# A hybrid backbone on one Trainium2 core: RMS norms folded into the transposes as diagonal products, two gathers' buffers exchanged, two steps moved, one add given to TensorE

## The chip, the cores and the metric

The kernel runs on one core of one Trainium2 chip. The metric is device time in microseconds from start to end of the program. All arithmetic is in 32-bit floats (fp32); the kernel's matrix products run either on fp32 operands or on pairs of fp32r operands (a rounded high part and a low part, three products per pair).

## The reference, cut to what matters

Two layers over 256 latent and 256 context tokens of width D = 1024. Each layer: a modulated RMS norm, one input projection that feeds three mixers, an output projection, a second modulated norm, and a mixture of 16 experts with two experts per token. In layer 1 the context tokens only feed the mixers.

```python
def rms_norm(x, g):
    return x * lax.rsqrt(jnp.mean(x * x, axis=-1, keepdims=True) + EPS) * g

for l in range(2):
    mod = jnp.split(silu(c) @ w_ada[l] + b_ada[l], 6)
    h  = rms_norm(x,  norm1_g[l]) * (1 + mod[1]) + mod[0]
    o  = token_mixers(h @ w_in[l], ...) @ w_out[l]
    x  = x + mod[2] * o
    h2 = rms_norm(x, norm2_g[l]) * (1 + mod[4]) + mod[3]
    x  = x + mod[5] * moe(h2)
```

The same is done to the context stream with `c_ctx` for `c`. The change touches `h`, the first norm of a layer, and in layer 1 what lies just ahead of it: the end of layer 0's experts, `x + mod[5] * moe(h2)`.

## The kernel before, in words

**Tiles.** The 512 tokens are four tiles of 128 (T = 0 to 3; 0 and 1 are latent, 2 and 3 context), held in SBUF as `X[T]`, 128 tokens by 1024 channels. To multiply by `w_in`, the channels must lie on the partitions, so each tile's eight 128x128 blocks (k-slices, ko = 0 to 7) are turned by TensorE.

**Opening of a layer.** `normed` (L397) goes over the tiles: ScalarE squares and sums the tile (L389), GpSimd (POOL) makes the mean plus epsilon (L391; in layer 0 VectorE does that) and its power -1/2, `rstd` (L394), and ScalarE writes the scaled tile `X * rstd` (L404) into the buffers `V` (tiles 0, 1), `UG` and `U`. `modulated` (L428) takes two k-slices of all four tiles: TensorE transposes them through `tr` (L181) into a PSUM tile `T`, ScalarE scales and shifts by the modulation (L440), VectorE casts the result to `big` and writes the low part (L190, L199). Then, per k-slice, `parts` splits the weight slice into `wsp` (ScalarE L189, VectorE L199) and 18 products (`mm3`, L157) add into the PSUM tiles `A`. This loop over ko (L455 to L485) makes the S5 and Fourier columns of the projection; in layer 1 it calls `modulated` at ko = 0 and 4, for two pairs of slices each, and loads half of the weight slices (`wload`, L303, 1 MB per half, on SP's DMA queue).

**Fillers.** `self.fill` is a generator of steps of `ada` (L306): each step k loads 1 MB of `w_ada` (L317) and multiplies it with the conditioning, four products into `E`. In layer 1 steps k < 5 load through GpSimd's queue, the later ones through SP's. The code calls `next(fill)` at set places: here in `ready(T)` of `combine0` (L1792), that is before each tile's norm (2, 1, 1, 1 steps), and in the ko loop after ko = 5.

**End of layer 0's experts.** In `experts0` each token's two expert rows are gathered from DRAM by GpSimd (L1684, two gathers of 0.5 MB per tile) into four buffers `rg[T]`; the order of the gathers in the code is T = 0, 1, 2, 3. The buffers come from three pools: `ws2`, the two `bm` buffers, and `ws`, the pool of four 1 MB buffers that also serves `w_in` and `w_ada`. Tile 3's is in `ws`. `others` (L1633 to L1637) and `back` then put gathered rows and modulated sums together; `back` is TensorE products of `y` with `OG`. The last loop (L1780) multiplies each tile's two PSUM halves `acc[T][n]` by the modulation `B5` and adds them to `X[T]` (L1789, L1790). For tile 3 VectorE first adds the gathered rows (L1788).

**What sets the order.** The Tile framework's scheduler places the instructions of each engine by its own model, apart from the stretches that `issue_after` and `chain` tie down; a buffer that is taken again from a pool makes its load wait for the last reader of the old contents. So an engine's order follows from program order, pools and that model together.

Of the kernel before, what the change touches and what calls it, by code (L numbers as in the profile page):

```python
# [19 lines left out]
P = 128  # L20
D = 1024
# [113 lines left out]
class Net:  # L135
# [261 lines left out]
    def normed(self, ready=None, pool=None):  # L397

        xv = self.t(self.mix, [P, 2, D], "V")
        self.xn = [xv[:, 0, :], xv[:, 1, :], self.t(self.mix, [P, D], "UG"), self.t(self.mix, [P, D], "U")]  # L400
        for T in range(4):
            if ready:
                ready(T)
            self.nc.scalar.activation(self.xn[T], self.X[T], AF.Copy, scale=self.rstd(T, pool=pool))  # L404


    def mixers(self, l, sa, sb):
# [20 lines left out]
        def modulated(kp):  # L428
            for s in range(2):
                xn = self.xn[2 * s:2 * s + 2]  # L430
                pt = t(self.psT, [P, 2, 256], "T")
                for i in range(2):
                    ko = 2 * kp + i
                    for sh in range(2):
                        self.tr(pt[:, i, sh * P:sh * P + P], xn[sh][:, ko * P:ko * P + P])
                f = t(self.tmp, [P, 2, 256], "w2")
# [19 lines left out]
        for ko in range(8):  # L456
# [21 lines left out]
            if both:  # L478
                if ko in (0, 2, 4):
                    next(self.first)  # L480
                    next(self.first)
                elif ko > 5:
                    next(fill)
            elif ko in (5,):
                next(fill)  # L485
# [1103 lines left out]
    def experts0(self, st):  # L1589
# [76 lines left out]
        for e in range(NE):  # L1666
# [12 lines left out]
            if e == NE - 1:  # L1679

                rg = [t(p, [P, 2048], "w").rearrange("p (k n) -> p k n", k=2) for p in (self.ws2, *self.bm, self.ws)]
                for T in range(4):
                    for k in range(2):
# [96 lines left out]
        for T in range(4):  # L1780
            if T == 3:
                back(0, 3)
            back(1, T)
            for n in range(2):
                c = slice(n * 512, n * 512 + 512)
                w = t(self.tmp, [P, 512], "w2")
                if T == 3:
                    nc.vector.tensor_add(w, acc[T][n], rg[T][:, 0, c])  # L1788
                nc.vector.tensor_mul(w, w if T == 3 else acc[T][n], B5[T // 2][:, c])  # L1789
                nc.vector.tensor_add(self.X[T][:, c], self.X[T][:, c], w)  # L1790

    def combine0(self):  # L1792

        def ready(T):
            for _ in range((2, 1, 1, 1)[T]):
                next(self.fill)
# [208 lines left out]
```

## Time and profile before

| What | us |
|---|---|
| median of 3 runs | 1094.84 |
| their range | 1093.45 to 1096.46 |
| time of the profiled execution | 1093.7 |
| its span, first to last instruction | 1091.9 |
| layer 0's opening | 0 to 63 |
| layer 0's mixers and routing | 63 to 340 |
| layer 0's experts | 340 to 640 |
| layer 1's opening, up to the next projection | 640 to 682 |
| layer 1's mixers and routing | 682 to 860 |
| layer 1's experts | 860 to 1092 |

TensorE (PE) is busy 1022.4 us (94% of the span), its weight loads (PEld) 649.7, VectorE (DVE) 598.1 (55%), ScalarE (ACT) 305.7 (28%), GpSimd (POOL) 164.0 (15%). The mean granted TensorE clock is 0.973 of full speed. A row of the timeline gives the start of an instruction or a run of like ones, their time and their count; in brackets stands how long the engine had been idle, and what released it. Ends of pipelined products overlap the next start, so a price is best read from start to start. An fp32 product counts as two records, a transpose as one.

### The profile page before, as it was taken

To read this page: it belongs to the slowest core of one execution; us is meant where nothing else is said; L and a number is where in the kernel's file an instruction comes from. 1 tells how busy PE (TensorE), PEld (TensorE's weight loads), DVE (VectorE), ACT (ScalarE), POOL (GpSimd) and SP (SyncE) were. 2 spreads that over 40 slices of the span, in tenths; PEclk is the share of its full clock that TensorE was granted. 3 is DMA by queue.
4 is the path that set the end of the run, shared out by engine and by line. 5 is a ranking of instruction groups with operands and counts; after the bars stand their busy time and mean duration, and the time that the engine had idled before them with its cause. 6 is when DMAs were issued, how large, how long until landed. Compare 5 with 4: busy or idle time off the path is not lost.

```text
span 1091.9 us, 21030 instructions
## 1 busy us (share of the span) xinstructions
PE 1022.4 (94%) x8468; PEld 649.7 (59%) x8468; DVE 598.1 (55%) x1675; ACT 305.7 (28%) x623; POOL 164.0 (15%) x259
## 2 busy tenths in 40 slices
PE   4999998989997999799999979999999999999997
PEld 2667676547895666465655528767658555555553
DVE  8987946657851322378663376784468423232232
ACT  5323234655101111010112244322373221111111
POOL 3101143001222321211111330113010000000000
PEclk9999999999977999999999998998999899999999
DMA  9867557757297999999999948634868999999991
GB/s 328 289 244 191 215 224 299 227 199 290 78 346 254 343 390 372 396 362 394 378 387 411 374 166 229 222 121 168 287 226 292 337 410 403 406 406 407 410 388 47
DMA packets 109121, 325.25 MB, mean 298 GB/s; under 512 B 10688, under 2 KB 19232, under 8 KB 104400
## 3 DMA queue, kind: packets, MB, share of 16 engines
q1 hardware_dynamic: 94016, 275.62, 68.3%
q0 software_dynamic: 14272, 46.96, 12.9%
q8 instruction: 71, 1.16, 0.4%
q10 hardware_dynamic: 720, 1.17, 0.3%
q14 instruction: 42, 0.34, 0.1%
HBM read 305.32 MB, written 18.38 MB: 296 GB/s over the span
## 4 chain that ended last, share of the span: by engine, by line
PE 43%; DMA 17%; DVE 4%; issue 3%; ACT 1%; POOL 1%; SPq 0%; ACTq 0%; DVEq 0%; POOLq 0%
DMA w<-in_w_up_dram 14%; PE g L157 13%; PE A L157 11%; PE D L157 7%; PE E L157 3%; PE u L157 3%; PE y L157 3%; PE T L181 2%; DMA w<-in_w_down_dram 1%; PE T L157 1%; DMA w<-in_w_ada_dram 1%; POOL qr L754 1%; PE T L1876 1%; DVE E L811 0%; ACT E L817 0%
## 5 line engine op out<-in xcount | busy, mean ns | idle before, releaser
L157 PE MATMUL A<-wsp,big 128*128 128x512 f32 (+1 forms) x720 | 163.8, 375 | 3.2 <-DVE big L190 2.1
L157 PE MATMUL g<-w,xt 128*32 128x384 f32 (+1 forms) x1280 | 149.5, 450 | 5.5 <-PEq L1533 3.2
L157 PEld LDWEIGHTS A<-wsp,big 128*128 128x128 f32 x720 | 122.8, 191 | 40.4 <-ACT wsp L189 7.5
L157 PE MATMUL u<-w,xt 128*32 128x384 f32 (+1 forms) x1024 | 121.2, 463 | 4.6 <-DMA w<-in_w_up_dram 4.6
L157 PEld LDWEIGHTS g<-w,xt 128*32 128x32 f32 x1280 | 68.1, 110 | 50.5 <-issue 26.6
L157 PE MATMUL g<-w,x 128*64 128x512 f32 x368 | 94.1, 595 | 0.0
L157 PE MATMUL y<-w,H 128*32 128x384 f32 (+1 forms) x1152 | 88.4, 456 | 5.7 <-issue 5.0
L157 PE MATMUL E<-w,CS 128*32 128x512 f32 (+1 forms) x448 | 60.4, 566 | 21.3 <-DMA w<-in_w_ada_dram 21.2
L157 PEld LDWEIGHTS y<-w,H 128*32 128x32 f32 x1152 | 52.8, 111 | 39.0 <-issue 18.0
L1946 DVE TENSOR_TENSOR cst<-cst,g 64x512 f32<-64x512 f32 x16 | 11.1, 691 | 117.6 <-ACT cst L1945 117.6
L199 DVE TENSOR_TENSOR wsp<-w,wsp 128x512 fp32r<-128x512 f32 x64 | 43.8, 687 | 50.8 <-ACT wsp L189 49.7
L157 PEld LDWEIGHTS u<-w,xt 128*32 128x32 f32 x1024 | 55.4, 111 | 25.8 <-ACT s L1714 2.9
L189 ACT ACTIVATE wsp<-w 128x512 fp32r<-128x512 f32 x64 | 40.2, 631 | 103.0 <-PE A L157 90.2
L157 PE MATMUL A<-w,big 128*128 128x512 f32 (+1 forms) x224 | 66.0, 386 | 0.0
L189 ACT ACTIVATE y<-y 96x384 f32<-96x384 f32 (+2 forms) x34 | 17.5, 516 | 155.2 <-PE y L157 99.8
L157 PEld LDWEIGHTS g<-w,x 128*64 128x64 f32 x368 | 29.9, 137 | 45.6 <-issue 42.2
L1709 DVE TENSOR_TENSOR s<-s,u 96x384 f32<-96x384 f32 x16 | 8.8, 551 | 85.0 <-ACT s L1708 85.0
L1618 POOL DMA_DIRECT2D xg<-G x60 | 32.6, 549 | 132.2 <-DVE xt L1625 77.9
L1901 DVE SCALAR_TENSOR_TENSOR y<-D,gs,ba 64x256 f32<-64x256 f32 x62 | 30.0, 483 | 38.2 <-PE D L157 37.4
L157 PE MATMUL D<-w,WO 128*64 128x256 f32 x384 | 47.2, 382 | 0.5 <-ACT WO L189 0.5
L157 PEld LDWEIGHTS A<-w,big 128*128 128x128 f32 x224 | 40.1, 188 | 7.6 <-issue 0.5
L157 PEld LDWEIGHTS D<-w,WO 128*64 128x64 f32 x384 | 28.7, 137 | 15.9 <-issue 2.6
(420 smaller groups left out, 1692.5 us busy)
## 6 DMA issues: line engine op xcount, KB each, us to landing
w<-in_w_gate_dram SPq DMA_DIRECT2D x110, 512.0 KB, 12.5
w<-in_w_up_dram SPq DMA_DIRECT2D x110, 512.0 KB, 12.4
w<-in_w_down_dram SPq DMA_DIRECT2D x55, 1024.0 KB, 12.6
w<-in_w_ada_dram SPq DMA_DIRECT2D x27, 1024.0 KB, 6.9
w<-in_w_in_dram SPq DMA_DIRECT2D x14, 1024.0 KB, 5.0
w<-in_w_ada_dram SPq DMA_DIRECT2D x32, 256.0 KB, 6.0
w<-in_w_ada_dram SPq DMA_DIRECT2D x16, 512.0 KB, 4.7
w<-in_w_out_dram SPq DMA_DIRECT2D x8, 1024.0 KB, 6.5
```

The source lines that it names most:

```text
L157: self.pe = self.pl = self.nc.tensor.matmul(out, lhsT, rhs, start=start, stop=stop)
L181: self.pl = self.nc.tensor.transpose(out, in_, self.ident[:n, :n])
L189: return self.nc.scalar.activation(out, in_, AF.Copy)
L199: self.lo = self.nc.vector.tensor_tensor(lo, x, hi.bitcast(F32), op=OP.subtract)
L754: nc.gpsimd.tensor_tensor(r, v, self.neghalf[:, 0:8], op=OP.pow)
L1618: q.dma_start(xg[blk(g)], rows[g])
L1709: nc.vector.tensor_mul(s[:cap, :], s[:cap, :], pg[1][:cap, 0:384])
L1876: nc.tensor.transpose(pt[:, k, :], s[64:P, k * P:k * P + P], self.ident[64:P, 64:P])
L1901: nc.vector.scalar_tensor_tensor(y[o:o + 64, m, b, :], py[m][q, :], gs[q, e % 2:e % 2 + 1], B5[q, m, :], op0=OP.mult, op1=OP.mult)
L1946: nc.vector.tensor_mul(s[64:P], s[64:P], pg[64:P])
```

## The change

There are five edits, in one diff:

1. `normed` no longer makes scaled tiles. GpSimd makes four diagonals `dg[T] = ident * rstd(T)`, 128x128 each, in the buffer `U`.
2. `modulated` replaces each transpose of a scaled block by an fp32 product of the block `X[T]` with `dg[T]`, which transposes and scales at once: 32 per layer, in both layers.
3. `ready(T)` takes one filler step for T = 0, 1, 2 and none for T = 3; the ko loop takes one after ko = 2, 4 and 6. In all there are six, as before.
4. Tile 2's gathered rows go to `ws` and tile 3's to the second `bm` buffer; the gathers are issued in the order 0, 1, 3, 2 of the code.
5. Tile 3's gathered rows are added in PSUM by two TensorE products with the identity, 128x512 each, instead of two VectorE adds.

```diff
--- before.py
+++ after.py
@@ -396,12 +396,12 @@
 
     def normed(self, ready=None, pool=None):
 
-        xv = self.t(self.mix, [P, 2, D], "V")
-        self.xn = [xv[:, 0, :], xv[:, 1, :], self.t(self.mix, [P, D], "UG"), self.t(self.mix, [P, D], "U")]
+        dg = self.t(self.mix, [P, 4, P], "U")
+        self.dg = [dg[:, T, :] for T in range(4)]
         for T in range(4):
             if ready:
                 ready(T)
-            self.nc.scalar.activation(self.xn[T], self.X[T], AF.Copy, scale=self.rstd(T, pool=pool))
+            self.nc.gpsimd.tensor_tensor(self.dg[T], self.ident, self.rstd(T, pool=pool).to_broadcast([P, P]), op=OP.mult)
 
 
     def mixers(self, l, sa, sb):
@@ -427,12 +427,12 @@
 
         def modulated(kp):
             for s in range(2):
-                xn = self.xn[2 * s:2 * s + 2]
                 pt = t(self.psT, [P, 2, 256], "T")
                 for i in range(2):
                     ko = 2 * kp + i
                     for sh in range(2):
-                        self.tr(pt[:, i, sh * P:sh * P + P], xn[sh][:, ko * P:ko * P + P])
+                        T = 2 * s + sh
+                        self.mm(pt[:, i, sh * P:sh * P + P], self.X[T][:, ko * P:ko * P + P], self.dg[T], True, True)
                 f = t(self.tmp, [P, 2, 256], "w2")
                 for i in range(2):
                     ko = 2 * kp + i
@@ -481,7 +481,7 @@
                     next(self.first)
                 elif ko > 5:
                     next(fill)
-            elif ko in (5,):
+            elif ko in (2, 4, 6):
                 next(fill)
         for T in range(4):
             self.cp(UT[:, T // 2, :, T % 2, :], pu[T // 2][:, T % 2, :].rearrange("p (g c) -> p g c", c=16))
@@ -1678,8 +1678,8 @@
                 xg = gather(e + 2)
             if e == NE - 1:
 
-                rg = [t(p, [P, 2048], "w").rearrange("p (k n) -> p k n", k=2) for p in (self.ws2, *self.bm, self.ws)]
-                for T in range(4):
+                rg = [t(p, [P, 2048], "w").rearrange("p (k n) -> p k n", k=2) for p in (self.ws2, self.bm[0], self.ws, self.bm[1])]
+                for T in (0, 1, 3, 2):
                     for k in range(2):
                         nc.gpsimd.indirect_dma_start(out=rg[T][:, k], out_offset=None, in_=self.Y,
                                                      in_offset=bass.IndirectOffsetOnAxis(ap=self.gi[:, k, T:T + 1], axis=0))
@@ -1780,19 +1780,19 @@
         for T in range(4):
             if T == 3:
                 back(0, 3)
+                for n in range(2):
+                    self.mm(acc[3][n], self.ident, rg[3][:, 0, n * 512:n * 512 + 512], False, False)
             back(1, T)
             for n in range(2):
                 c = slice(n * 512, n * 512 + 512)
                 w = t(self.tmp, [P, 512], "w2")
-                if T == 3:
-                    nc.vector.tensor_add(w, acc[T][n], rg[T][:, 0, c])
-                nc.vector.tensor_mul(w, w if T == 3 else acc[T][n], B5[T // 2][:, c])
+                nc.vector.tensor_mul(w, acc[T][n], B5[T // 2][:, c])
                 nc.vector.tensor_add(self.X[T][:, c], self.X[T][:, c], w)
 
     def combine0(self):
 
         def ready(T):
-            for _ in range((2, 1, 1, 1)[T]):
+            if T < 3:
                 next(self.fill)
         self.normed(ready, self.fin)
         self.finx.close()
```

**TensorE, layer 1's opening, before.** `y<-y,OG` is the last product of `back`; `E` are the filler steps (x4 is one step), `T` the transposes, `A` the projection.

```order
L157 MATMUL E_10218<-w_10221,CS_95 32x512 x4
L157 MATMUL E_10218<-w_10227,CS_95 32x512 x4
L157 MATMUL E_10218<-w_10241,CS_95 32x512 x4
L181 MATMUL T_10295<-cst_5_87,V_10215 128x128 x4
L157 MATMUL E_10218<-w_10255,CS_95 32x512 x4
L181 MATMUL T_10305<-cst_5_87,UG_10216 128x128
L181 MATMUL T_10315<-cst_5_87,V_10215 128x128 x4
L157 MATMUL E_10218<-w_10269,CS_95 32x512 x4
L181 MATMUL T_10305<-cst_5_87,U_10217 128x128
L181 MATMUL T_10305<-cst_5_87,UG_10216 128x128
L181 MATMUL T_10305<-cst_5_87,U_10217 128x128
L157 MATMUL A_10289<-wsp_2072_10335,big_2054_10284 128x256
```

The same place after the change, first up to the first `A`:

```order
L157 MATMUL y_2016_10144<-w_10009,cst_5_87 128x512
L157 MATMUL y_2017_10145<-w_10009,cst_5_87 128x512
L157 MATMUL y_2016_10144<-y_10134,OG_9715 128x512
L157 MATMUL y_2017_10145<-y_10134,OG_9715 128x512
L157 MATMUL E_10214<-w_10217,CS_95 32x512 x4
L157 MATMUL E_10214<-w_10231,CS_95 32x512 x4
L157 MATMUL E_10214<-w_10245,CS_95 32x512 x4
L157 MATMUL T_10279<-U_10213,X_1_66 128x128 x4
L157 MATMUL T_10289<-U_10213,X_2_67 128x128
L157 MATMUL T_10299<-U_10213,X_1_66 128x128 x4
L157 MATMUL A_10273<-wsp_2066_10319,big_2048_10268 128x256
```

Eleven `A` products on, at the last `A` of ko = 1 for tiles 0 and 1:

```order
L157 MATMUL A_10273<-wsp_2068_10341,big_2049_10269 128x256
L157 MATMUL E_10214<-w_10385,CS_95 32x512 x4
L157 MATMUL E_10214<-w_10477,CS_95 32x512 x4
L157 MATMUL T_10289<-U_10213,X_2_67 128x128 x3
L157 MATMUL T_10309<-U_10213,X_2_67 128x128 x4
```

The products with the identity (`y<-w,cst`) stand ahead of the last two of `back`. Filler steps 0 to 2 are followed by the blocks of tiles 0 and 1 for both pairs of slices and by twelve `A` products on them; steps 3 and 4, which stood between the transposes, now stand behind those, and the blocks of tiles 2 and 3 behind them.

**GpSimd, layer 1's opening, before** (`w<-in_w_ada_dram` at L317 are loads of filler steps 3 and 4; steps 0 to 2 stand ahead of this):

```order
L391 TENSOR_SCALAR var_10250<-ss_10248 128x1
L394 TENSOR_TENSOR rstd_10252<-var_10250,neghalf_98 128x1
L317 DMA w_10255<-in_w_ada_dram 128x2048
L391 TENSOR_SCALAR var_10264<-ss_10262 128x1
L317 DMA w_10269<-in_w_ada_dram 128x2048
L394 TENSOR_TENSOR rstd_10266<-var_10264,neghalf_98 128x1
L391 TENSOR_SCALAR var_10278<-ss_10276 128x1
L394 TENSOR_TENSOR rstd_10280<-var_10278,neghalf_98 128x1
L1058 DMA MT_9212<-KD_1890_9208 16x16x128 x8
```

The same place after the change:

```order
L404 TENSOR_TENSOR U_10213<-cst_5_87,rstd_10228 128x128
L404 TENSOR_TENSOR U_10213<-cst_5_87,rstd_10242 128x128
L515 DMA qkg_10569<-in_qkg_dram 128x128
L391 TENSOR_SCALAR var_10254<-ss_10252 128x1
L394 TENSOR_TENSOR rstd_10256<-var_10254,neghalf_98 128x1
L404 TENSOR_TENSOR U_10213<-cst_5_87,rstd_10256 128x128
L317 DMA w_10385<-in_w_ada_dram 128x2048
L391 TENSOR_SCALAR var_10262<-ss_10260 128x1
L317 DMA w_10477<-in_w_ada_dram 128x2048
L394 TENSOR_TENSOR rstd_10264<-var_10262,neghalf_98 128x1
L1058 DMA MT_9210<-KD_1888_9206 16x16x128
L404 TENSOR_TENSOR U_10213<-cst_5_87,rstd_10264 128x128
```

The load of step 3 stood behind the second tile's `rstd`; it now stands behind two more diagonals and the third tile's `rstd` and diagonal. Step 4's load stands behind it, one `var` apart, as before. On SP's queue the first half of `w_in` for layer 1 takes over the `ws` buffer of tile 2's rows: its load waited for TensorE's filler step 2 there, and waits for VectorE's add of tile 2's gathered rows (L1637) now; the second half waited for L1788's read of tile 3's rows, and waits for filler step 1.

## Rows read from the trace of the kernel before

**Rows 1.** Windows of core 0 in layer 1's opening: busy us by engine, clock, DMA share, GB/s

```profile
646.00:650.00 4.00, 0.82 (x8) 0.16 (x8) 2.73 (x8) 3.79 (x8) 2.97 (x6) 1.00 0.94 376
650.00:655.00 5.00, 0.94 (x9) 0.53 (x5) 0.01 (x1) 1.39 (x3) 3.50 (x7) 0.94 1.05 392
655.00:661.00 6.00, 5.28 (x24) 3.61 (x25) 2.67 (x5) 2.41 (x5) 0.56 (x1) 0.50 1.06 164
```

**Rows 2.** Chain that ended last: start us, us, what

```profile
646.74 8.94 DMA w<-in_w_ada_dram
```

**Rows 3.** Timeline of PE, layer 1's opening: start us, us, instruction, count, idle before

```profile
642.50 2.78 PE L157 MATMUL E<-w,CS 128*32 128x512 f32 x24
645.21 0.66 PE L181 MATMUL T<-cst,V 128*128 128x128 f32 x4
649.18 1.07 PE L157 MATMUL E<-w,CS 128*32 128x512 f32 x8 [3.31 <-DMA w<-in_w_ada_dram]
655.72 1.94 PE L157 MATMUL E<-w,CS 128*32 128x512 f32 x8 [4.78 <-DMA w<-in_w_ada_dram]
...
658.14 2.06 PE L157 MATMUL A<-wsp,big 128*128 128x256 f32 x8
...
669.79 1.05 PE L157 MATMUL E<-w,CS 128*32 128x512 f32 x2
```

**Rows 4.** Timeline of POOL over the same stretch, same columns

```profile
643.90 0.60 POOL L317 DMA_DIRECT2D w<-in_w_ada_dram  x1
...
649.49 4.01 POOL L1058 DMA_DIRECT2D MT<-KD  x7
```

**Rows 5.** Timeline of SP's DMA queue and of ACT there, same columns

```profile
645.34 0.92 SPq L303 DMA_DIRECT2D w<-in_w_in_dram  x2
642.91 2.20 ACT L404 ACTIVATE V<-X,rstd 128x1024 f32<-128x1024 f32 x2
646.18 1.02 ACT L440 ACTIVATE w<-T,MC,A 128x256 f32<-128x256 f32 x2
654.33 1.15 ACT L189 ACTIVATE wsp<-w 128x512 fp32r<-128x512 f32 x2 [3.61 <-DMA w<-in_w_in_dram]
```

**Rows 6.** Timeline of DVE: adds of other experts' rows, tiles 2 and 3

```profile
630.66 2.35 DVE L1637 TENSOR_TENSOR X<-X,w 128x1024 f32<-128x1024 f32 x2
642.88 0.68 DVE L1788 TENSOR_TENSOR w<-y,w 128x512 f32<-128x512 f32 x1
```

**Rows 7.** Timeline of PE: prices of a transpose and of a product

```profile
638.97 3.60 PE L157 MATMUL y<-y,OG 96*128 96x512 f32 x8
...
669.14 0.27 PE L181 MATMUL T<-cst,UG 128*128 128x128 f32 x1
669.25 0.27 PE L181 MATMUL T<-cst,U 128*128 128x128 f32 x1
...
773.00 1.16 PE L157 MATMUL A<-WB,cst 128*128 128x128 f32 x8
```

**Rows 8.** Groups of POOL's instructions over the run: count, busy us, mean ns, idle before

```profile
L370 POOL TENSOR_TENSOR A<-A,n 128x8 f32<-128x8 f32 x2 | 0.4, 202 | 0.2
L394 POOL TENSOR_TENSOR rstd<-var,neghalf 128x1 f32<-128x1 f32 x8 | 5.0, 626 | 5.0 <-DVE usq L968 1.2 <-DVE tn L941 1.2 <-DVE usq L967 1.2
```

**Rows 9.** Windows of layer 0's opening, columns as in the first group

```profile
20.00:30.00 10.00, 8.93 (x74) 6.00 (x73) 9.11 (x36) 3.65 (x10) 1.06 (x5) 1.00 1.07 386
30.00:40.00 10.00, 9.14 (x70) 5.75 (x68) 9.77 (x22) 2.89 (x6) 0.63 (x1) 1.00 0.82 275
40.00:50.00 10.00, 9.65 (x78) 6.95 (x77) 9.10 (x16) 3.32 (x8) 1.46 (x3) 1.00 0.89 304
50.00:60.00 10.00, 9.79 (x80) 7.43 (x75) 8.91 (x15) 3.75 (x8) 2.13 (x4) 1.00 0.77 277
```

**Rows 10.** Timeline of PE and ACT in layer 0's opening: the first wait

```profile
23.14 0.51 PE L157 MATMUL A<-wsp,big 128*128 128x256 f32 x2 [1.02 <-DVE big L190]
...
21.04 1.93 ACT L440 ACTIVATE w<-T,MC,A 128x256 f32<-128x256 f32 x4 [0.41 <-POOL A L370]
```

## The prediction

> **What bounds the kernel now.** I read the page first: TensorE is busy 94% of the span, so time is won only where it waits, runs slowly, or has less to do. Then I read the windows and TensorE's timeline around the two places that the change touches.
>
> In layer 1's opening TensorE stands still. [rows 3] show two waits, both for `w_ada` loads: 3.31 us ahead of filler step 3 at 649.18, 4.78 us ahead of step 4 at 655.72. The chain that ended last [rows 2] agrees: it goes through the load of step 4, 8.94 us from its issue at 646.74. The windows [rows 1] show the second half of the loss. TensorE was busy 0.82 of 4 and 0.94 of 5 us, and then, from 655 to 661, its granted clock is 0.50, the lower of its two levels (1.2 instead of 2.4 GHz). The 5.28 us of work there would take about 2.6 at 1.00.
>
> Why the load is late is in [rows 4, 5]. Between 643.90 and 646.74 four loads of 1.05 MB are issued: step 3, both halves of `w_in`, step 4. From 643.90 to 655.72 these are 4.2 MB in 11.8 us, an average of 356 GB/s, with the `MT` transfers behind them from 649.49 on. Also, the projection cannot start before ScalarE has split `w_in`, and its first half is there at 654.33.
>
> In layer 0's opening [rows 9] no single wait dominates. From 20 to 60 us TensorE is busy 8.93, 9.14, 9.65 and 9.79 of each 10, 2.5 us idle in all, while VectorE is busy 91 to 98%. [rows 10] show the first of these waits, 1.02 us for VectorE's cast behind ScalarE's L440.
>
> **Prices.** A transpose of 128 columns costs 0.11 from start to start (669.14 to 669.25, [rows 7]). The change's product was not in the trace before. Nearest below: an fp32 product of 512 columns is 0.88 (four in 3.53 us, 638.97 to the next at 642.50, [rows 7, 3]), a quarter is 0.22. Nearest above: four fp32 products of 128x128 in 1.16 with the last one's end, 0.29. I take 0.22, since the 1.16 holds a pipeline's end. So each replaced transpose costs 0.11 more (at most 0.18): 32 per layer are 3.5 us (at most 5.8). The Trainium skill, TensorE: Matmul & The Clock Gate, Terms, gives transpose mode as four times faster for fp32, which speaks against this edit; these rows show a factor of two, and by the page's factor 32 products would add some 10 us (an estimate from the page) where the rows give 3.5.
>
> **Layer 1, step by step, as a difference at the end of the opening.**
> - *Loads.* The first half of `w_in` no longer waits at 645.34; its buffer is free when VectorE ends L1637 at 633.0 [rows 6], when the DMA stands nearly idle. The second half waits for filler step 1. Two products with the identity stand ahead of it, 2 x 0.88 = 1.8, so step 1 ends near 642.50 + 1.8 + 2 x 0.92 = 646.1 (three steps take 2.78, [rows 3]). Step 3 is issued behind two more diagonals and the third tile's norm, near 646.9, 3.0 later than at 643.90. Step 4 follows near 647.8, 1.1 later. So 3.15 MB go from 646.0 on; at 356 GB/s that is 8.9 us and step 4 lands at 654.9, **0.8 earlier**. At 392 GB/s [rows 1] it would be 654.1; if the `MT` transfers are in the way as before, step 4 slips by its own 1.1, to 656.8.
> - *Twelve projection products* for tiles 0 and 1 now stand ahead of steps 3 and 4 and run inside the wait, since half of `w_in` is there. A product is 0.13 at full clock (eight in 2.06 at half clock, [rows 3]): **-1.5**.
> - *Clock.* With these, and with nine products of twice a transpose's length, TensorE works some 2.5 us more (1.0 and 1.5) between 646 and 652 than before, and its remaining waits are near 2 us each. I take it to stay at the higher level: **-2.6**. Other end: 0.
> - *Products instead of transposes* behind step 4: 7 of the first group and 16 later, 23 x 0.11 = **+2.5** (at most 4.1). The nine ahead lie in the wait.
> - *A new wait.* Tiles 2 and 3 come only behind step 4, and the next projection products need them through L440 (1.02 for a pair, [rows 5]) and VectorE's cast. Before, products of tiles 0 and 1 covered that; these are used up. **+1.1** (0 to 2).
> - *VectorE* loses two adds of 0.68 [rows 6] and *ScalarE* four scalings of 1.1 [rows 5]. Neither ends the wait; they are covered by the loads and cost and gain nothing. If the cover went (loads by 650), the norm of tile 3 would be what is late.
> - *Step moved to ko = 2 and 4*: TensorE's order already has both ahead of them; step 5, whose products stood at 669.79 without a wait [rows 3], is loaded later among the `MT` transfers. 0, at most 2.
>
> Sum: -0.8 - 1.5 - 2.6 + 2.5 + 1.1 = **-1.3** (from -3.2 to +3).
>
> *The diagonals* are 128x128 multiplications on GpSimd. The trace has 0.20 for 128x8 and 0.63 for the power on one column [rows 8]; between 0.2 and 1 each is possible, and I take 0.4, since the operation is the cheap one of the two on more elements. That is in the 3.0 of step 3. At 1 us each, step 3 would come 1.8 later still. The Trainium skill, GPSIMD Engine Reference, 3.1, puts a two-operand elementwise operation at about 2.6 cycles per element against VectorE's 1, which points upward; no row here shows it.
>
> **Layer 0.** The same 3.5 us of extra TensorE time enter a stretch with 2.5 us of TensorE idle. If all of it could be filled, 1.0 remains; if none, 3.5, and 5.8 at the high price. VectorE, as busy and with unchanged work, sets part of the pace, so I stay near the low end: **+1.7**. The four scalings saved on ScalarE lie before 19 us, where TensorE waits for the filler's weights, and win nothing. In the order ScalarE's weight splits now come behind L440's four, which holds the first projection products by up to 0.5; that is in the 1.7.
>
> **Sum.** -1.3 + 1.7 = **+0.4** on the profiled execution's own 1093.7, that is 1094.1. The median of the runs stands 1.1 above that execution, so I forecast 1095.2. Some 0.3%, 3.3 us, is what a measurement of this kernel tells from no change, so this is no change.
>
> **The rivals.**
> 1. *The stall goes and layer 0 hides its part.* Loads at 392 GB/s (-1.6) and no new wait in L440 give -1.6 - 1.5 - 2.6 + 2.5 = -3.2 in layer 1; if VectorE is the pace of layer 0, its price falls to 0 to 1. Time 1091.6 to 1092.6. For it: VectorE's 98% in one window. Against: TensorE is 97 to 98% busy in two others. Chance 0.20; about 0.17 in all is beyond 0.3%, with what the moved orders further down may bring.
> 2. *The clock falls all the same* (the other side). Two waits remain. If the clock falls behind the second of them as it did before, the work behind runs at half clock as before, and layer 1 is +1.3 instead of -1.3: +3.0 with layer 0, 1097.9. It decides whether the window behind step 4 has 0.50 or 1.00. For it: those windows [rows 1] were at 1.00 and 0.94 until the second wait. Against: less waiting. The Trainium skill, TensorE: Matmul & The Clock Gate, Part 4, says that transpose mode does not count as busy for the clock, which speaks against this rival, as products replace it; the trace agrees in so far as the clock fell behind a stretch of steps and transposes, but waits were there too. Chance 0.22.
> 3. *Layer 0 pays in full*: no idle time can be filled, since each wait hangs on the very products that got longer. +3.5 to +5.8 there, 1097.0 to 1099.3. For it: the wait in [rows 10] begins with these products. Chance 0.15.
> 4. *The change doesn't shorten the loads*: step 3's load is three us later, meets `MT`, and step 4 lands at 656.8 instead of 654.9. +1.9 more, 1097.1. Chance 0.13.
>
> **The numbers.** My own case has 0.30. The range 1091.2 to 1099.0 takes in rivals 2 and 4, rival 3 up to nearly its high price and rival 1 almost whole. Faster by over 0.3% needs rival 1 and more: 0.17. Slower by over 0.3% (beyond 1098.1) needs rival 3's upper half or rival 2 with a dearer layer 0: 0.23. The rest, 0.60, is within 0.3%.
>
> **What would show it.** Right: product starts 0.22 apart; the first `w_in` half issued at 633 and split before 648; two waits of about 2 us at steps 3 and 4, granted clock 1.00 behind them; layer 1's projection starting a microsecond earlier relative to the end of the experts; layer 0's opening ending 1 to 2.5 us later. Wrong: a window at 0.50 behind step 4 (rival 2), a wait at step 5, diagonals near 1 us, or a difference outside both openings, which I have nothing for.

## The result: slower by 0.65%, and the profile after

The change runs in 1102.92 us (median of 8 runs, 1100.65 to 1104.58), the kernel before in 1095.55 (8 runs, 1093.24 to 1099.35). The ratio is 1.0065, 95% interval 1.005 to 1.008. I had forecast 1095.2 and no change; 1102.92 lies outside the range. The profiled execution took 1103.0 (span 1101.2), 9.3 more than that of before.

The page's first lines after the change: TensorE's busy time is up by 13.3 us from 1022.4, VectorE's by 0.8 from 598.1, though it has two adds less. ScalarE's falls by 7.9.

```profile
span 1101.2 us, 21163 instructions
...
PE 1035.7 (94%) x8536; PEld 661.8 (60%) x8536; DVE 598.9 (54%) x1673; ACT 297.8 (27%) x615; POOL 166.3 (15%) x267
```

Laid over each other, the two executions part in the two openings. At 128 us the change is 5.3 behind. At the last L1633, near the end of layer 0's experts, it is 5.2 behind (639.71 against 634.49), at 748 us 11.4, from 835 on 9.7. The 1.7 that it makes good at the end lie in layer 1's mixers, where no edit is; there the other execution, that of before, had its clock at 0.50 from 745 to 750 us.

**Layer 1's opening, TensorE after** (it answers to [rows 3]; `y<-w,cst` are the products with the identity, `T<-U,X` those with the diagonals):

```profile
645.90 1.88 PE L157 MATMUL y<-w,cst 128*128 128x512 f32 x4
...
649.44 2.78 PE L157 MATMUL E<-w,CS 128*32 128x512 f32 x24
...
654.42 1.16 PE L157 MATMUL T<-U,X 128*128 128x128 f32 x8 [0.89 <-ACT w L440]
655.33 1.73 PE L157 MATMUL A<-wsp,big 128*128 128x256 f32 x12
660.40 1.94 PE L157 MATMUL E<-w,CS 128*32 128x512 f32 x8 [3.34 <-DMA w<-in_w_ada_dram]
664.63 1.93 PE L157 MATMUL E<-w,CS 128*32 128x512 f32 x8 [2.29 <-DMA w<-in_w_ada_dram]
...
669.25 2.07 PE L157 MATMUL T<-U,X 128*128 128x128 f32 x8 [1.11 <-ACT w L440]
```

The order is the one forecast: twelve `A` products, then two waits for steps 3 and 4, then a wait for L440. The waits for the loads, 3.34 and 2.29, were forecast near 2 each. But step 4 starts 15.19 us behind step 0 (664.63 against 649.44); it was 13.22 before [rows 3], and my 654.9 meant 10.6 (step 0 at 642.50 + 1.8).

The windows of the same stretch (they answer to [rows 1]) show the two reasons, the rate in the last column and the clock two before it:

```profile
651.00:653.00 2.00, 2.00 (x19) 0.98 (x12) 1.99 (x6) 1.34 (x3) 1.80 (x3) 1.00 0.56 46
653.00:655.00 2.00, 1.11 (x10) 0.92 (x10) 0.75 (x4) 1.02 (x2) 1.75 (x4) 1.00 0.80 289
655.00:657.00 2.00, 2.00 (x18) 1.86 (x16) 0.55 (x1) 0.00 (x0) 1.98 (x5) 1.00 1.09 337
657.00:659.00 2.00, 0.06 (x1) 0.00 (x0) 0.00 (x0) 0.00 (x0) 2.00 (x4) 1.00 0.94 348
659.00:661.00 2.00, 0.60 (x4) 0.20 (x8) 0.00 (x0) 0.00 (x0) 0.40 (x2) 0.83 0.98 406
661.00:663.00 2.00, 1.34 (x8) 0.00 (x0) 0.00 (x0) 0.00 (x0) 0.20 (x1) 0.50 1.06 264
663.00:665.00 2.00, 0.37 (x4) 0.20 (x8) 0.00 (x0) 0.00 (x0) 0.14 (x1) 0.50 1.10 137
665.00:667.00 2.00, 2.00 (x10) 0.51 (x3) 0.00 (x0) 0.00 (x0) 0.43 (x1) 0.50 1.06 141
```

The granted clock is down at 0.50 (1.2 of 2.4 GHz) from 661 on, behind 2 us in which TensorE worked 0.06 and 2 more in which it worked 0.60. And the rate, 46 GB/s in the first window, is 289 to 348 for 6 us, 406 for 2, and then 264 and 137, though the DMA engines are full (1.06 and 1.10). Where the loads stood in the queues, POOL first (it answers to [rows 4]):

```profile
652.57 0.40 POOL L404 TENSOR_TENSOR U<-cst,rstd 128x128 f32<-128x128 f32 x1
653.09 0.62 POOL L317 DMA_DIRECT2D w<-in_w_ada_dram  x1
...
654.02 0.58 POOL L317 DMA_DIRECT2D w<-in_w_ada_dram  x1
...
655.21 0.63 POOL L1058 DMA_DIRECT2D MT<-KD  x1
```

and SP's queue, with the two halves of `w_in` ([rows 5] before), whose row spans both issues, the first at 638.31, the second near 651.4:

```profile
638.31 13.48 SPq L303 DMA_DIRECT2D w<-in_w_in_dram  x2
```

With the 5.2 that layer 1 starts later, I had forecast 638.2 and 651.3 for the halves (they came there), and 652.1 and 653.0 for steps 3 and 4: both are 1.0 late. The first `MT` transfer is issued 1.2 us behind step 4; before it was 2.75 (649.49 against 646.74, [rows 4, 2]).

**Layer 0's opening, TensorE after** (it answers to [rows 9, 10]):

```profile
18.97 2.03 PE L157 MATMUL T<-U,X 128*128 128x128 f32 x16
20.93 1.05 PE L157 MATMUL E<-w,CS 128*32 128x256 f32 x10
23.36 0.35 PE L157 MATMUL A<-wsp,big 128*128 128x256 f32 x1 [1.37 <-DVE big L190]
24.40 0.38 PE L157 MATMUL A<-wsp,big 128*128 128x256 f32 x1 [0.69 <-DVE big L190]
...
34.02 1.95 PE L157 MATMUL T<-U,X 128*128 128x128 f32 x16
35.90 0.63 PE L157 MATMUL E<-w,CS 128*32 128x256 f32 x4
```

Eight products (16 records) take 1.88 from start to start, 0.235 each, against the forecast 0.22 and 0.11 for a transpose [rows 7].

**A ledger of the openings.** I cut each opening in parts, the same way for every kernel. Waits are the sum of the brackets on TensorE's rows. Half clock is the sum over one-us windows of TensorE's busy time times what the granted clock lacks to 1. The rest is what remains: work at full speed, and stalls that the rows don't show as idle time. Layer 0 runs from the first transposes of the modulation (`T<-cst,ba`, 18.50 after) to the first `A` product of 512 columns on 128 partitions:

| layer 0's opening, us | length | waits | half clock | rest |
|---|---|---|---|---|
| before | 44.65 | 2.29 | 0 | 42.36 |
| change | 50.24 | 2.24 | 1.70 | 46.30 |
| edits 1, 2 in layer 0 alone | 48.38 | 1.90 | 0 | 46.48 |
| the same, products made twice | 54.33 | 1.57 | 0 | 52.76 |
| the same, weight splits first | 47.55 | 2.14 | 0 | 45.41 |
| unscaled tiles transposed | 48.56 | 4.40 | 0 | 44.16 |
| layer 0 as before, 12 other kernels | 45.0 to 48.5 | 2.6 to 3.6 | 0 to 3.2 | 41.9 to 42.4 |

Layer 1 runs from the last L1633 to the next such product; the second column is the way from there to filler step 0, which the rest leaves out here:

| layer 1's opening, us | length | to step 0 | waits | half clock | rest |
|---|---|---|---|---|---|
| before | 47.20 | 8.01 | 8.09 | 2.76 | 28.34 |
| change | 54.39 | 9.73 | 7.63 | 5.06 | 31.97 |
| change, layer 0 as before | 52.33 | 9.73 | 8.34 | 1.75 | 32.51 |
| the same, steps 3, 4 on SP | 51.91 | 9.72 | 5.67 | 2.86 | 33.65 |
| edits 3, 4, 5 | 47.35 | 9.73 | 5.28 | 2.19 | 30.15 |
| edit 4 alone | 42.73 | 8.00 | 3.01 | 3.04 | 28.68 |
| edit 5 alone | 47.88 | 9.73 | 4.18 | 5.59 | 28.38 |
| edits 4, 5 | 47.74 | 9.73 | 7.31 | 2.86 | 27.84 |
| edit 4, edits 1, 2 in layer 1 | 48.16 | 8.01 | 5.62 | 2.20 | 32.33 |
| edit 4, tile 2 scaled by VectorE | 40.79 | 8.01 | 3.46 | 0.00 | 29.32 |
| layer 1 as before, 4 other kernels | 47.0 to 49.3 | 8.0 | 7.7 to 9.3 | 3.0 to 4.0 | 28.2 to 28.4 |

So in the profiled executions layer 0 cost 5.6 (3.9 of work, 1.7 of half clock) and layer 1 cost 7.2: 1.7 for the identity's products, 3.6 of other work, 2.3 of half clock, and 0.5 less of waits. The last rows of the tables are kernels with the same code in that layer (for layer 1 the four that change layer 0 alone). Their rest and their way to step 0 hardly differ, while waits and half clock do from one execution to the next. So the added work on TensorE is the change's; the 1.7 of half clock in layer 0 and the 2.3 in layer 1 are not shown to be.

### The profile page after: what moved, and what is told of

It is laid out like the page before. It is cut to its first block, busy times and chain, and to the rows that moved or that the text cites. A ratio compares the mean times of both kernels' runs of the same rounds, so it can differ in the third digit from the quotient of the medians.

```text
span 1101.2 us, 21163 instructions
## 1 busy us (share of the span) xinstructions
PE 1035.7 (94%) x8536; PEld 661.8 (60%) x8536; DVE 598.9 (54%) x1673; ACT 297.8 (27%) x615; POOL 166.3 (15%) x267
## 4 chain that ended last, share of the span: by engine, by line
PE 48%; DMA 11%; DVE 5%; issue 2%; ACT 1%; POOL 1%; SPq 0%; ACTq 0%; DVEq 0%; POOLq 0%
PE g L157 15%; PE A L157 10%; PE D L157 6%; DMA w<-in_w_up_dram 6%; PE u L157 5%; DMA w<-in_w_gate_dram 4%; PE y L157 4%; PE E L157 3%; PE T L181 2%; PE T L157 2%; DMA w<-in_w_ada_dram 1%; POOL qr L754 1%; PE T L1876 1%; DVE E L811 0%; ACT E L817 0%
## 5 line engine op out<-in xcount | busy, mean ns | idle before, releaser
L157 PE MATMUL u<-w,xt 128*32 128x384 f32 (+1 forms) x1024 | 124.1, 464 | 4.1 <-DMA w<-in_w_up_dram 2.9
## 6 DMA issues: line engine op xcount, KB each, us to landing
w<-in_w_gate_dram SPq DMA_DIRECT2D x110, 512.0 KB, 12.7
```

Source lines behind the costliest of these rows:

```text
L157: self.pe = self.pl = self.nc.tensor.matmul(out, lhsT, rhs, start=start, stop=stop)
```

## The experiments

Edits are numbered as in the section on the change; ratios are to the kernel before on the same chip, whose medians in the four batches were 1095.26, 1096.68, 1094.91 and 1096.75 us. Letters in the quoted expectations are theories; what came of each is said in the text.

### Which half of the change costs

**The change without layer 0, and layer 0 alone.** The first keeps layer 0 as before, with its scaled tiles. The second makes edits 1 and 2 in layer 0 and nothing else (the same switch the other way round, on the kernel before). The core of the first, against the change:

```diff
+                if l == 1:
...
+                            self.mm(pt[:, i, sh * P:sh * P + P], self.X[T][:, ko * P:ko * P + P], self.dg[T], True, True)
+                else:
+                    xn = self.xn[2 * s:2 * s + 2]
...
+                            self.tr(pt[:, i, sh * P:sh * P + P], xn[sh][:, ko * P:ko * P + P])
```

> The changed kernel, but layer 0 scales and transposes as before. Theory A (layer 0 alone costs 5.3 us, read as the shift of both traces at 94 to 290 us): 1097.7 us beside 1102.9 for the change, ratio to before about 1.002 to 1.004, and layer 1's opening unchanged against the change (step 4 lands some 3.6 us late, 0.50 behind it). Rival (the shift is one of the two executions, not of layer 0): within 1.5 us of the change.

> The kernel before with edits 1 and 2 in layer 0 alone. Theory A: +5.3 us, ratio 1.005, with the products' 3.5 us and a stretch of about 4 us at granted clock 0.50 behind 25 us, since the weight splits come behind L440. Rival (only the products' price, the clock fell by chance): +3.5 us, ratio 1.003, clock 1.00 from 20 to 40 us.

Measured: 1097.98, ratio 1.0032 [1.0014, 1.005], and 1098.92, ratio 1.0026 [1.0008, 1.0043]. Each half costs about 0.3%, and together they make the whole. Layer 0 pays some 3.6 us (1.0065 less 1.0032), twice what I took. The lower clock that theory A expected in layer 0 alone did not come (half clock 0). Of the 4.0 us of longer products the ledger finds 4.1 in the rest. It has 0.4 less of waits than before's own profile, and 0.9 to 1.2 less than the mean of 3.1 in the 13 profiles with layer 0 as before, when all three kernels with edits 1 and 2 and single products there are taken (1.90 to 2.24).

**Single edits of layer 1.** Edit 4 alone (the gathers' buffers), edit 3 alone (the steps), both, and edit 5 alone (the identity), as the diff of the change has them; that of edit 4, on the kernel before:

```diff
-                rg = [t(p, [P, 2048], "w").rearrange("p (k n) -> p k n", k=2) for p in (self.ws2, *self.bm, self.ws)]
-                for T in range(4):
+                rg = [t(p, [P, 2048], "w").rearrange("p (k n) -> p k n", k=2) for p in (self.ws2, self.bm[0], self.ws, self.bm[1])]
+                for T in (0, 1, 3, 2):
```

> The kernel before with edit 4 alone (tile 2's rows in the weights' pool, order of the gathers). The load of step 3 now takes the buffer that tile 2's rows free near 633 us. Theory B (loads that are issued late set layer 1's opening): three instead of four loads meet in the 644 to 656 us stretch, step 4 lands near 652 to 653 us and the time falls by 2 to 4 us, ratio 0.997. Rival (the MT transfers set when step 4 lands, or the clock takes it back): within 1 us of before.

> The kernel before with edit 3 alone (the two moved steps). In TensorE's order twelve A products now stand ahead of step 3. Theory B (the moved steps as such cost nothing; the loads do): within 1.5 us of before. Rival (the moved steps are what costs layer 1 its time, since A products that wait for the first half of w_in now stand ahead of step 3): slower by 3 us or more, ratio 1.003 to 1.005.

> Edits 3 and 4 on the kernel before. Theory C (the gain of edit 4 alone is that step 3's load takes the early buffer; with the moved steps the first half of w_in takes it, and steps 3 and 4 load late): the gain of 5.7 us is gone, 1093 to 1097 us. Rival (any early load helps as much): 1088 to 1091 us.

> Edit 5 alone on the kernel before. The last reader of tile 3's rows is now a TensorE product. Theory G (the two products with the identity lie on the path for their 1.7 us and shift the filler steps and the loads behind them): slower by 1.5 to 4 us, ratio 1.0015 to 1.0035. Rival (two VectorE adds less end the norm of tile 3 earlier by as much): within 1 us of before.

| kernel | median | ratio [95%] |
|---|---|---|
| edit 4 | 1089.56 | 0.9945 [0.9924, 0.9966] |
| edit 3 | 1093.55 | 0.9983 [0.9969, 0.9998] |
| edits 3, 4 | 1089.17 | 0.993 [0.9909, 0.9952] |
| edit 5 | 1095.87 | 1.0011 [0.9998, 1.0024] |

Edit 4 alone is faster, and edit 3 does not take that back: the theory (C) that the moved steps steal the buffer that edit 4 frees fell here. The first half of `w_in` does take it in edits 3 and 4 (632.09), and the gain stays. With edit 4 the load of filler step 3 goes out while the DMA stands idle, and that of step 4 ahead of `w_in`. POOL of edit 4 alone:

```profile
634.65 0.53 POOL L317 DMA_DIRECT2D w<-in_w_ada_dram  x1 [10.33 <-DVE X L1637]
...
645.24 0.60 POOL L317 DMA_DIRECT2D w<-in_w_ada_dram  x1
```

Its SP queue:

```profile
645.83 1.23 SPq L303 DMA_DIRECT2D w<-in_w_in_dram  x2
```

On its TensorE four steps (x32) run without a break, and no wait for a load is left ahead of step 4:

```profile
643.84 3.64 PE L157 MATMUL E<-w,CS 128*32 128x512 f32 x32
...
650.29 0.33 PE L181 MATMUL T<-cst,UG 128*128 128x128 f32 x1 [2.22 <-ACT UG L404]
650.55 1.06 PE L157 MATMUL E<-w,CS 128*32 128x512 f32 x8
```

In the change that early buffer goes to the first half of `w_in` instead (638.31 there), and both steps' loads come later.

Edit 5 alone costs nothing that can be told (theory G fell). It has the 1.72 us of the two products with the identity on the way to step 0, but 3.9 less of waits than before. In its order both steps' loads go out ahead of `w_in`, step 4's at 647.64 and `w_in` at 648.12, and step 4's products start 7.1 us behind step 0 (646.14), where before they started 13.2 behind:

```profile
647.64 0.58 POOL L317 DMA_DIRECT2D w<-in_w_ada_dram  x1
```

```profile
648.12 1.23 SPq L303 DMA_DIRECT2D w<-in_w_in_dram  x2
```

```profile
653.21 1.93 PE L157 MATMUL E<-w,CS 128*32 128x512 f32 x8 [1.52 <-DMA w<-in_w_ada_dram]
```

### What takes the gain back

**Edit 4 with edit 5, and with edits 1 and 2 in layer 1.**

> Edits 4 and 5 on the kernel before. Theory C: step 3's load stays early, two products with the identity add at most 1.8 us to TensorE: 1089.5 to 1091.5 us. Rival D (the identity products push every later issue back and cost as much as the swap gains): 1093 us or more.

> Edits 1 and 2 in layer 1, and edit 4; no moved step, no identity product. Theory C: as with edit 4 alone or up to 2 us either way, 1087.5 to 1091.5 us, since the diagonals end the wait of 2.2 us for ScalarE's scaled tile that edit 4 alone shows, and the products give 3.5 us back. Rival E: 1093 us or more.

Measured: 1095.22, ratio 0.999 [0.9971, 1.0009], and 1094.7, ratio 0.9991 [0.9971, 1.0011]. Either takes back most of the 0.55% (0.45 and 0.46, 4.9 and 5.0 us). The products with the identity are 1.72 us of TensorE, which the ledger finds in the way to step 0. And step 4's load has another place: POOL of edits 4 and 5 issues it at 646.18, behind the third tile's norm and behind `w_in` on SP at 645.78, and TensorE stands 5.69 us for it:

```profile
646.18 0.60 POOL L317 DMA_DIRECT2D w<-in_w_ada_dram  x1
```

```profile
645.78 1.23 SPq L303 DMA_DIRECT2D w<-in_w_in_dram  x2
```

```profile
653.82 1.94 PE L157 MATMUL E<-w,CS 128*32 128x512 f32 x8 [5.69 <-DMA w<-in_w_ada_dram]
```

With the diagonals instead, step 4 is issued behind two of them, at 645.40, 0.1 behind `w_in` (645.31), and TensorE waits 3.73 for it. In three kernels, then, step 4's products start 6.7 us behind step 0 where its load goes out ahead of `w_in`, 9.7 and 10.0 where behind. That goes together in all three, and edit 5 alone (ahead, 7.1 us) and the change without edit 3 further down (behind, 12.7) agree; a kernel that turns that order alone was not run.

**The change in layer 1 without edit 3, and without edits 1 and 2.** Both have layer 0 as before: the first is edits 1, 2, 4 and 5 in layer 1, the second edits 3, 4 and 5, with lines of the diff of the change and no others.

> The change without the moved steps, with layer 0 as before: edits 1, 2, 4 and 5 in layer 1. Theory C: step 3's load is issued near 634 us and the time is 1089 to 1093 us, against 1098.0 with the moved steps. Rival E (products in place of transposes, and the diagonals on GpSimd, cost layer 1 its time): 1095 us or more.

> Edits 3, 4 and 5 on the kernel before, that is the change without diagonals in either layer. Theory H (the two products with the identity shift all behind them by 1.7 us, and the products in place of transposes cost layer 1 3.5 us and the loads' delay behind the diagonals): 1091 to 1093.5 us, ratio 0.996 to 0.998. Rival (edit 5 is covered as the VectorE adds were): 1088.5 to 1090.5 us as with edits 3 and 4.

Measured: 1098.18, ratio 1.002 [1.0003, 1.0037], and 1093.18, ratio 0.9973 [0.9956, 0.9991]. Without the diagonals the change in layer 1 is a gain, with them a loss of 0.32%. Built up in steps, edits 3 and 4 give -0.70%, edit 5 on top +0.43%, edits 1 and 2 in layer 1 +0.59%, in layer 0 +0.33%: together +0.65%, the result. (The single steps are differences between batches, each uncertain by about 0.25%.)

**The loads taken off GpSimd's queue.** In the change with layer 0 as before, and in edits 3 and 4, steps 3 and 4 load through SP, where no diagonal and no `MT` stands ahead:

```diff
-            (q if q and k < 5 else nc.sync).dma_start(w, A["w_ada"][l][k * P:k * P + P, sc * 2048:sc * 2048 + 2048])
+            (q if q and k < 3 else nc.sync).dma_start(w, A["w_ada"][l][k * P:k * P + P, sc * 2048:sc * 2048 + 2048])
```

> The change with layer 0 as before, and filler steps 3 and 4 loaded through SP's queue instead of GpSimd's, where the diagonals and norms stand ahead of them. Theory F (those loads are late because they stand behind the diagonals on GpSimd): both are issued about 2 us earlier against the first filler step, 1093 to 1096 us instead of 1098.0. Rival (the products' and the identity's own TensorE time, 5.2 us, is the cost): 1097 us or more.

> Edits 3 and 4 on the kernel before, with filler steps 3 and 4 loaded through SP's queue. Theory F: steps 3 and 4 come 1 to 2 us earlier than with edits 3 and 4 alone and the waits of 0.2 and 1.25 us for them go: 1086.5 to 1089 us, faster than before by 0.7%. Rival (the wait for VectorE's cast, 2.5 us, and the MT transfers set it): 1089 to 1091 us.

Measured: 1098.52, ratio 1.0029 [1.0018, 1.0041], where the kernel without it had 1.0032; and 1091.49, ratio 0.9967 [0.9956, 0.9979], against 0.993: no gain in the one, a loss in the other. The theory (F) that the queue behind the diagonals is the cost fell. The waits for steps 3 and 4 are nearly gone in the first, but the stall goes on to the next load, step 5, and the clock falls there instead:

```profile
653.88 1.05 PE L157 MATMUL E<-w,CS 128*32 128x512 f32 x2 [0.80 <-DMA w<-in_w_ada_dram]
...
670.37 1.92 PE L157 MATMUL E<-w,CS 128*32 128x512 f32 x2 [3.98 <-DMA w<-in_w_ada_dram]
```

```profile
670.00:674.00 4.00, 3.63 (x10) 1.97 (x11) 0.23 (x1) 0.00 (x0) 0.00 (x0) 0.50 0.81 320
```

### Layer 0: price or order

Three kernels with layer 1 as before: the tiles of layer 0 transposed unscaled (the first norm's scaling is left out); edits 1 and 2 in layer 0 with every product made twice; and the same with single products but the first two weight slices split ahead of L440.

```diff
+        if not ready:
+            self.xn = self.X
...
```

```diff
+                            self.mm(pt[:, i, sh * P:sh * P + P], self.X[T][:, ko * P:ko * P + P], self.dg[T], True, True)
+                            self.mm(pt[:, i, sh * P:sh * P + P], self.X[T][:, ko * P:ko * P + P], self.dg[T], True, True)
```

```diff
+                if ko == 0:
+                    pre = [parts(w[0]), parts(w[1])]
...
-            p = parts(w[ko])
+            p = pre[ko] if both and ko < 2 else parts(w[ko])
```

> The kernel before, but in layer 0 the unscaled tiles are transposed (the first norm's scaling is left out there; no scalings, no diagonals, plain transposes). ScalarE's order is that of the change, weight splits behind L440. Theory A1 (layer 0's 3.3 us is the price of 32 products of about 0.12 us more each, none of it absorbed): the time of before, within 1.2 us, 1094 to 1097 us. Rival (the order on ScalarE and the late weight splits cost it): 1097.5 us or more.

> Edits 1 and 2 in layer 0 alone, with each of the 32 products done twice into the same place (no part of the result is left out). Price theory (layer 0's opening is paced by TensorE's own work): 32 times 0.22 to 0.24 more, 7 to 7.7 us more than with one product each, ratio 1.008 to 1.010. Order theory (ScalarE's late weight splits set the time, products are covered): within 3 us of one product each, ratio up to 1.0055.

> Edits 1 and 2 in layer 0 alone, with the weight splits of the first two k-slices written ahead of the first blocks; they come behind the first L440 on ScalarE instead of the fourth. Order theory: half or more of layer 0's cost goes, ratio at most 1.0015. Price theory: the wait of 1 us at the first product falls by at most 0.7 us, ratio 1.002 to 1.003.

Measured: 1098.16, ratio 1.0029 [1.0013, 1.0045]; 1106.12, ratio 1.0077 [1.0048, 1.0106]; 1098.46, ratio 1.0021 [1.0, 1.0043]. The second set of products costs 0.51% more than the first alone (uncertain by about 0.3%), 5.6 us, and 6.3 in the ledger's rest: what is added to TensorE here is paid nearly in full, and the waits give back 0.3. Splitting the weights first changes nothing that can be told (1.0021 against 1.0026). Its interval reaches 1.0, so some share of the late splits is not excluded; that they are the main cost has nothing for it. The unscaled tiles went against the theory of the price (A1) as I had written it: with no longer product the kernel is as slow as with them. Its first projection product waits 2.20 us for a split of ScalarE's:

```profile
23.57 0.56 PE L157 MATMUL A<-wsp,big 128*128 128x256 f32 x2 [2.20 <-ACT wsp L189]
```

Waits rise to 4.40 and the rest by 1.8, though its 32 transposes take 3.97 us from start to start, as before (3.91; the products 7.59). I read this as another, worse order of the opening's instructions; why it is worse was not looked for. In its profile 3.3 us more are lost behind the opening, where no edit is (7.2 behind at the last L1633, 3.9 over the opening), so its time can't be put on the opening alone. How much of the first 32 products' cost would be order in the same way is not settled by that; that it is work on TensorE is what the ledger and the doubled products say.

### The version that beats both

In edit 4 alone TensorE still waits 2.22 us for ScalarE's scaling of tile 2, which takes 1.15 there. VectorE does that one scaling in 0.75; the edit, on top of edit 4 and in layer 1 only:

```diff
+            if ready and T == 2:
+                self.nc.vector.tensor_scalar(self.xn[T], self.X[T], self.rstd(T, pool=pool), None, op0=OP.mult)
+                continue
             self.nc.scalar.activation(self.xn[T], self.X[T], AF.Copy, scale=self.rstd(T, pool=pool))
```

> Edit 4 alone, with layer 1's scaling of tile 2 done by VectorE instead of ScalarE. The wait of 2.2 us for ScalarE's scaled tile that edit 4 alone shows should shrink by about 1 us and tile 3's by 0.6: 1087.5 to 1089 us, ratio 0.993. Rival (VectorE's casts are pushed back by the 1.2 us, or the loads are next): 1089 to 1091 us, ratio 0.9945.

Measured: 1086.95, ratio 0.9912 [0.9884, 0.9941], the fastest of all. Its TensorE, and windows of the same stretch:

```profile
642.65 3.64 PE L157 MATMUL E<-w,CS 128*32 128x512 f32 x32
...
648.70 0.33 PE L181 MATMUL T<-cst,UG 128*128 128x128 f32 x1 [1.83 <-DVE UG L405]
```

```profile
646.00:650.00 4.00, 2.08 (x20) 0.99 (x16) 3.42 (x9) 2.36 (x6) 2.24 (x4) 1.00 0.90 364
650.00:654.00 4.00, 2.37 (x18) 1.30 (x11) 1.36 (x3) 3.22 (x6) 4.00 (x8) 1.00 1.07 419
654.00:658.00 4.00, 4.00 (x36) 4.00 (x35) 3.77 (x7) 2.49 (x5) 1.14 (x2) 1.00 1.05 266
```

The wait is only 0.4 shorter, but the clock stays at 1.00, and the ledger's half clock falls from 3.04 to nothing. Against edit 4 alone the intervals overlap, so the last 0.3% is not shown; against both kernels of the case it is faster.

## Why the prediction was wrong, step by step

In short: my sum drew gains of 0.8 from earlier loads, 1.5 from products inside the wait and 2.6 from the clock, and let part of the longer products vanish in idle time. In the ledger of layer 1, waits and half clock together went up by 1.8 against before's profile instead, and the work added to TensorE was paid for the most part.

**Layer 1's loads, -0.8: the step that failed first.** Measured from the last L1633, step 4 starts 24.92 us on (664.63 less 639.71), 21.23 before: +3.7. The queues' order and the times of both halves of `w_in` were right. The issues of steps 3 and 4 were 1.0 late each, since what stands ahead of them on POOL took longer than I had added up. The larger part, 3.5, is the time of the transfers. I gave 3.15 MB 8.9 us, at an average of 356 GB/s; they took 13.2, from 651.4 to 664.6.

The 356 was a wrong reading to begin with. It counts 4.2 MB as landed when step 4 starts in the kernel before, but the core had moved 3.7 MB by then, 314 GB/s, since the second half of `w_in` was still on its way (it landed 21.4 us behind its issue):

```profile
643.90:655.72 11.82, 3.73 (x33) 1.28 (x25) 5.56 (x14) 7.76 (x12) 7.06 (x14) 0.94 0.92 314
```

At 314 my 8.9 us are 10.0. After the change the average is 272 over the 13.2 us. It starts at 46 in the first window above, goes up to 406, and is 131 in the last 2.6 us. In those last 2.6 us the packets are small ones, 118 of 121 under 8 KB, while the loads of steps 3 and 4 go in packets of 8 KB:

```profile
DMA packets 121, 0.34 MB, mean 131 GB/s; under 512 B 40, under 2 KB 40, under 8 KB 118
```

So the `MT` transfers, issued 1.2 us behind step 4 in the same queue, can have held step 4 in that stretch only. My rival 4 named them, and their nearness was mine to read off from POOL's order; but no run took `MT` away, so how much of the 2.6 us is due to them stays open. Part of the +3.7 is also the luck of before's own profile: in the four other kernels with layer 1 as before step 4 starts 21.8 to 23.8 us behind the last L1633. The change is later than all of them, so the forecast of 0.8 earlier stays wrong.

**Twelve projection products in the wait, -1.5: right in the order.** They run at 655.33, ahead of the wait of 3.34. That they saved 1.5 no run shows by itself.

**The clock, -2.6: wrong.** It fell to 0.50 from 661 to 673, longer than before; the ledger has 5.06 where I had expected none and before had 2.76. Rival 2 had it. But the excess over before is not shown to be the change's: with the same layer 1 and layer 0 as before it was 1.75, and layer 1 as before had 2.76 to 3.98 in five profiles. What failed is the gain of 2.6, which did not come. The Trainium skill, TensorE: Matmul & The Clock Gate, Part 4, does not count transposes as busy for the clock in the same way. The runs here don't sort by that, nor by the longest wait: with products the clock fell behind waits of 3.34 and 2.29; with transposes it stayed at 1.00 in the fastest kernel, where no wait was above 1.83, and fell in edit 5 alone, where the waits up to there were 0.97 and 1.52:

```profile
654.00:656.00 2.00, 2.00 (x13) 0.93 (x6) 0.77 (x2) 0.00 (x0) 0.94 (x2) 0.50 0.49 104
```

**Products behind step 4, +2.5, and the wait for L440, +1.1.** The second is exact (1.11 at 669.25); a first one of 0.89 at 654.42 I hadn't seen. The products are 0.125 dearer each, 4.0 for 32. My step let nine vanish in the wait, which takes the wait's end as fixed. The ledger has the price of all 32 in the rest: 3.6 above before in the change, and 3.65 where edits 1 and 2 in layer 1 come on top of edit 4 (32.33 against 28.68). The waits are only 0.5 less in the change and 2.6 more in the other. That norms and loads' buffers hang on the same chain would explain it; it was not tested.

**The identity's products: not in the sum.** I used their 1.8 us only to shift the loads. They stand ahead of filler step 0, on the engine that sets the pace, and ahead of the reads that release the buffers for the next loads. On top of edits 3 and 4 they cost 0.43%, 4.7 us, more than their own time; alone 0.11%, not to be told from nothing. That their cost hangs on the order of the loads behind them agrees with both; no run turned that order alone. The two VectorE adds that they replace gave no gain that shows.

**Layer 0, +1.7: mis-sized.** It measured 2.8 (alone) to 3.6 us (within the change) by the runs. I let half of the price go into 2.5 us of idle time, beside a VectorE that I took for busy to 91% and more (the last of [rows 9] has 89). By the ledger 0.4 went, against before's own profile, or about 1, against the mean of the 13; of the doubled products 0.3. Rival 3 had the size; its reason, that each wait hangs on the products that got longer, fits and was not tested apart.

**The diagonals, 0.4: right**, as the group of POOL's rows shows:

```profile
L404 POOL TENSOR_TENSOR U<-cst,rstd 128x128 f32<-128x128 f32 x8 | 3.0, 393 | 0.1
```

**The chances.** Rivals 2, 3 and 4 came all together. I had priced each alone, at chances of 0.22, 0.15 and 0.13, as if only one could hold. Added to my own sum, with 2.6 for the clock, 3.5 - 1.7 for layer 0 and 1.9 for the loads, they give 1095.2 + 2.6 + 1.8 + 1.9 = 1101.5, close to the result. That closeness is partly luck: the 1.9 is less than the loads' measured miss, and the identity's 1.7 is in none of them. They are not independent: a later load makes a longer wait, and in this profile the clock fell behind the waits. Adding them was the step left out.

## What to carry to other kernels

Work moved onto the engine that sets the pace was paid here for the most part, though idle time stood beside it (2.8 to 3.6 of 4.0 us, 5.6 of the next 6.3): before counting idle time as room, ask what each wait hangs on. Products put ahead of the last read of a buffer delay the load that is to take it; what that cost differed with the loads' order (edit 5 alone cost nothing that can be told, on top of edit 4 it cost 4.9 us). A rate read from issue to use counts only what has landed by then. Try such edits one by one: here one of five was a gain of 0.55%, most of which either of two others took back. Rivals that can come together (a later load, a longer wait, a lower clock) are to be summed as one case with its own chance.

## What the runs showed of the hardware that I had not expected

**A lower clock that belongs to no edit.** After the change, layer 0's opening had a stretch at half clock:

```profile
24.00:26.00 2.00, 1.60 (x8) 1.29 (x9) 2.00 (x5) 0.00 (x0) 0.00 (x0) 0.86 1.06 407
26.00:28.00 2.00, 2.00 (x9) 1.81 (x9) 1.79 (x10) 0.00 (x0) 0.00 (x0) 0.50 1.07 382
```

Such a stretch, worth about 1.7 us (3.2 in one), is there in 9 of 13 profiles of kernels whose layer 0 is that of before; the profile of before itself is among the four without. One profile of each kernel can't tell that from an effect; the medians can.

**VectorE beside GpSimd.** While GpSimd makes the diagonals of layer 0,

```profile
14.22 1.46 POOL L404 TENSOR_TENSOR U<-cst,rstd 128x128 f32<-128x128 f32 x4
```

VectorE's four small multiplications under way take 0.39 to 0.43 each. One of them:

```profile
14.93 0.43 DVE L884 TENSOR_TENSOR ca<-RO,unit 128x16 f32<-128x16 f32 x1
```

In the kernel before, with no diagonals made, the same instruction took 0.18:

```profile
14.29 0.18 DVE L884 TENSOR_TENSOR ca<-RO,unit 128x16 f32<-128x16 f32 x1
```

It is off the path here, some 1 us in all, but VectorE's time has a share in the price of such a diagonal.
